# Two more weight sums of a seven-product pair made by accumulating DMAs, and the last convolution written stage by stage

## The chip, the cores and the metric

The kernel runs on one core of one Trainium2 chip. The metric is the device time of one execution in microseconds (us); lower is better. The engines named below are TensorE (PE; PEld is its weight load), VectorE (DVE), ScalarE (ACT), GpSimd (POOL) and SyncE (SP), which only issues transfers. Each engine runs its own instructions in order. Transfers issued by SP and by POOL go through separate queues and are carried by the same 16 DMA engines.

## The reference: what is computed

One decoder layer on x of 256 tokens by 2048 columns, all float32. The part that the change touches is the channel mixer: an up-projection to 2 x 5632 columns, a causal depthwise convolution of width 3, a gated GELU, and the down-projection.

```python
def causal_dwconv(u, w, b):
    S = u.shape[1]
    up = jnp.pad(u, ((0, 0), (CONV_WIDTH - 1, 0), (0, 0)))
    y = b
    for kk in range(CONV_WIDTH):
        y = y + up[:, kk:kk + S] * w[kk]
    return y
...
        x = x + rmsnorm(mix, post_mix_g[l])
        h = rmsnorm(x, pre_ffn_g[l])
        u = causal_dwconv(h @ w_up[l], conv_w[l], conv_b[l])
        gate, val = jnp.split(u, 2, axis=-1)
        y = (jax.nn.gelu(gate, approximate=True) * val) @ w_down[l]
        x = x + rmsnorm(y, post_ffn_g[l])
```

Ahead of it stand the pre-norm, the input projection (`w_in`), two groups of attention heads and the output projection (`w_out`).

## The kernel before

**Three matmuls for one.** Every float32 weight that is loaded into a `raw` buffer is split: ACT writes a rounded copy (`hi`), then DVE subtracts it from the weight (`lo`). A product of float32 accuracy is three matmuls: activation-high by `hi`, activation-high by `lo`, activation-low by `hi`. So each loaded unit of 128 x 1024 weights costs one ACT instruction, one DVE instruction and a pair of output tiles (`whi`/`wlo`, `slots`, or `more`, in which the second half of the layer has eight more places).

**Stages.** Attention and the projections around it fill the first 325 us or so. Then the feed-forward part runs in two halves of 22 blocks of 128 hidden columns. A half is a gate/up stage (11 groups g; for each the gate and the value columns are projected from `w_up`, convolved, passed through GELU, multiplied and split into the tiles `G`) and two column passes, which multiply the 22 blocks by columns 0 to 1023 and 1024 to 2047 of `w_down` (c0 is 0 or 1024). So there are four column passes.

**Seven products.** A pass goes over pairs u of blocks (k, k+1). Six of the eleven pairs (`FAST`) are done by seven products where eight are usual, as in Strassen's method in Winograd's form: tokens in two halves, the block pair as two rows, 512 columns each, so the weights form b11, b12 (row k, left and right) and b21, b22 (row k+1). With t1 = b11 + b12, t3 = b22 + b12, t2 = b22 + t1 and t4 = b21 + t2 the seven products multiply the tiles b11, (t1, t3), (b21, b22) and (t2, t4). A seven-product pair takes 7 x 3 = 21 matmuls of 512 columns, a plain pair 24.

**Where the sums come from.** t1 and t3 are made in DRAM long ahead, in a tile `t13` per pair: two copies from `w_down` by SP, then two accumulating transfers by POOL that add b12. These four steps per pair are put into the stream of weight loads by `w_load` (one step at every fifth load after the twelfth). In the pass itself `prepare` loads b11, (t1, t3) as `r13` and row k+1 as `r2`; (t2, t4) is then made on DVE by two additions of 128 x 512 over `r13` (L1025 and L1026), which wait for the split of `r13` to be done, and whose result is split in its turn.

**Order.** PE is ordered by hand everywhere. In the last group of a half and in the passes ACT, DVE and SP also go in the order of the code; elsewhere a scheduler orders them. A pass runs its pairs in a fixed order, for example 0, 2, 4, 1, 5, 6, 7, 3, 8, 9, 10 in the last one. After the last seven-product pair `early_sums` (L1141 to L1149) turns four accumulators into output columns: one ACT copy and eight DVE additions in the second half. The last pairs of a pass are held back and are multiplied bank by bank (`block`), and after each bank in the second half `down` (L1209, L1210) adds it on DVE and squares it on ACT.

**Convolution.** `conv_begin` (L921 to L929) takes for one block of 128 channels: an ACT copy, a DVE addition, a POOL multiplication, an ACT activation. `conv_end` has two DVE instructions. In the last group of a half it runs for the two value blocks one after the other, after the splits of the pass's first two plain pairs have been put in line.

Of the kernel before, what the change touches and what calls it, by code (L numbers as in the profile page):

```python
# [17 lines left out]
P = 128  # L18
S = 256
D = 2048  # L20
# [4 lines left out]
NEG = -1e30  # L25
FHALF = 22
HOLD = 3
EVERY, SKIP = 5, 12
FAST = (0, 2, 4, 5, 6, 7)


# [1 line left out]
def hybrid_layer(ctx: ExitStack, tc: tile.TileContext, x, pre_mix_g, w_in, b_forget, sinks,  # L33
# [33 lines left out]

    pair_sums, sum_steps, loads, paused = {}, [], [0], [False]

    def make_sums(key, k):  # L70
        t = tc.dram_tile([P, D], F32, name="t13")
        pair_sums[key] = t
        to = t.rearrange("p (s x c) -> p s x c", s=2, x=2)
        ups, downs = (w_down[(k + a) * P:(k + a + 1) * P, :]
                      .rearrange("p (s x c) -> p s x c", s=2, x=2) for a in range(2))
        return [lambda: sp.dma_start(to[:, :, 0, :], ups[:, :, 0, :]),
                lambda: sp.dma_start(to[:, :, 1, :], downs[:, :, 1, :]),
                lambda: pool.dma_start(to[:, :, 0, :], ups[:, :, 1, :], accum_op=ALU.add),
                lambda: pool.dma_start(to[:, :, 1, :], ups[:, :, 1, :], accum_op=ALU.add)]

    def w_load(src, a, c, pin=False):
        raw = wp.tile([P, UNIT], F32, tag="raw", bufs=5, name="raw")
        i = sp.dma_start(raw[:, :a * c].rearrange("p (a c) -> p a c", a=a), src)
        if pin:
            tc.keep_in_program_order(i)
        loads[0] += 1
        if loads[0] % EVERY == 0 and loads[0] > SKIP and sum_steps and not paused[0]:
            tc.keep_in_program_order(sum_steps.pop(0)())
        return raw, a, c

    for half in range(2):
        for u in FAST:
            sum_steps += make_sums((half, u), half * FHALF + 2 * u)


    LOW = 56

# [770 lines left out]
    with tc.tile_pool(name="ffn", bufs=1) as fp:  # L868
# [45 lines left out]
        y_sb = main.tile([P, 2, D], F32, tag="y", name="y_sb")  # L914

        def conv(b, ch, dst_tag):
            return conv_end(*conv_begin(b, ch, dst_tag))

        def conv_begin(b, ch, dst_tag):
            u = ubuf[cnt[0] % NU]  # L920
            cnt[0] += 1  # L921
            c = from_ring("cs")
            act.copy(c, b[:, 256:512])
            dve.tensor_tensor(u[:, 2:258], b[:, 0:256], c, op=ALU.add)  # L924
            pool.tensor_tensor(u[:, 2:258], u[:, 2:258], rowf, op=ALU.mult)  # L925
            y = from_ring(dst_tag)
            act.activation(y, u[:, 2:258], AF.Identity, bias=cw[:, 3, ch:ch + 1],  # L927
                           scale=cw[:, 2, ch:ch + 1])
            return u, y, ch  # L929
# [71 lines left out]
        def column_pass(G, sums, weights, some, order, k00, c0, load, parts, hold=1):  # L1001

            left, right = slice(0, 512), slice(512, UNIT)
            fast = [u for u in order if u in some]
            plain = [u for u in order[:-hold] if u not in some]
            ready, started, held, banks = {}, set(), [], []
# [9 lines left out]
            def prepare(u):  # L1016
                k = k00 + 2 * u
                if u not in some:
                    return [parts(load(w_rows(w_down, k + a, 1, c0, UNIT)), UNIT)
                            for a in range(2)]  # L1020
                b11 = parts(load(w_rows(w_down, k, 1, c0, 512)), 512)
                r13 = load(weights[u][:, c0:c0 + UNIT].rearrange("p (a c) -> p a c", a=1))
                r2 = load(w_rows(w_down, k + 1, 1, c0, UNIT))
                f13 = parts(r13, UNIT)
                dve.tensor_tensor(r13[:, left], r2[:, right], r13[:, left], op=ALU.add)  # L1025
                dve.tensor_tensor(r13[:, right], r2[:, left], r13[:, left], op=ALU.add)  # L1026
# [126 lines left out]
        for half in range(2):  # L1153
# [5 lines left out]
            for g in range(FHALF // 2):  # L1159
# [18 lines left out]
                if g == FHALF // 2 - 1:  # L1178
                    inner = tc.manual_schedule(engines={mybir.EngineType.Activation,
                                                        mybir.EngineType.DVE,  # L1180
                                                        mybir.EngineType.SP})
                    inner.__enter__()
                    passes = column_passes()
                    passes[0][0](1, 3)
                    begun = [conv_begin(bv[m], 44 + c0 // P + m, "yv") for m in range(2)]
# [142 lines left out]
```

## Time and profile before

| | |
|---|---|
| time, median of 3 runs (lowest to highest) | 1075.53 us (1075.0 to 1076.7) |
| time of the profiled execution | 1075.73 us |
| its span, first to last instruction | 1074.0 us |
| mean granted TensorE clock | 0.996 |
| busy: PE, DVE, ACT, POOL | 1048.1, 856.1, 647.6, 249.1 us |
| bytes moved by DMA | 238.56 MB, mean 222 GB/s |
| gate/up stage and two passes of the first half | from about 365 to 580 us, 580 to 695 us |
| gate/up stage and two passes of the second half | from 695 to 938 us, 938 to about 1064 us |

A row of the profile's groups reads: line, engine, operation, what is written and read, number of instructions, then busy time in us and mean ns of one, then the idle time of the engine just before them and what ended it. A row of a timeline reads: start, duration, engine, line, operation; in brackets the idle time before it and its releaser. A row of windows gives for a stretch of time the length, the busy time of each engine with the number of instructions in brackets, the clock granted to PE (1.00 is full), the busy share of the DMA engines and the GB/s. A matmul of 512 columns is listed with some 390 ns because matmuls overlap.

### The profile page before, as it was taken

To read this page: it belongs to the slowest core of one execution; us is meant where nothing else is said; L and a number is where in the kernel's file an instruction comes from. 1 tells how busy PE (TensorE), PEld (TensorE's weight loads), DVE (VectorE), ACT (ScalarE), POOL (GpSimd) and SP (SyncE) were. 2 spreads that over 40 slices of the span, in tenths; PEclk is the share of its full clock that TensorE was granted. 3 is DMA by queue.
4 is the path that set the end of the run, shared out by engine and by line. 5 is a ranking of instruction groups with operands and counts; after the bars stand their busy time and mean duration, and the time that the engine had idled before them with its cause. 6 is when DMAs were issued, how large, how long until landed. Compare 5 with 4: busy or idle time off the path is not lost.

```text
span 1074.0 us, 16449 instructions
## 1 busy us (share of the span) xinstructions
PE 1048.1 (98%) x5866; PEld 906.8 (84%) x5866; DVE 856.1 (80%) x1389; ACT 647.6 (60%) x1116; POOL 249.1 (23%) x280
## 2 busy tenths in 40 slices
PE   9999999999999999999999999999999999999895
PEld 7899988888889888888888787888888888878574
DVE  5988878887468788788776999867778887689895
ACT  7776757767457666566564656555556565565661
POOL 3253344440131122222221000012222222100005
PEclk9999999999999999999999999999999999999998
DMA  8749688675984998777876767768787766658482
GB/s 293 238 132 226 186 233 248 185 218 157 328 271 112 318 269 235 218 235 222 246 215 167 260 240 248 226 215 230 235 235 227 210 203 194 196 176 282 151 322 86
DMA packets 171230, 238.56 MB, mean 222 GB/s; under 512 B 8044, under 2 KB 132236, under 8 KB 170252
## 3 DMA queue, kind: packets, MB, share of 16 engines
q1 hardware_dynamic: 163616, 222.25, 64.6%
q0 software_dynamic: 6528, 12.58, 7.9%
q10 hardware_dynamic: 1004, 2.68, 0.6%
q8 instruction: 46, 0.75, 0.3%
q14 instruction: 36, 0.29, 0.1%
HBM read 233.14 MB, written 29.38 MB: 244 GB/s over the span
## 4 chain that ended last, share of the span: by engine, by line
PE 74%; DVE 13%; issue 5%; ACT 4%; DMA 2%; POOL 1%; SPq 0%; DVEq 0%; ACTq 0%; POOLq 0%
PE bank_acc L305 14%; PE bank_att L305 13%; PE bank_acc L330 12%; PE bank_acc L311 7%; PE bank_acc L274 7%; PE bank_att L311 7%; PE bank_acc L279 4%; PE bank_att L998 4%; DVE wlo L334 3%; DVE more L334 2%; DMA raw<-in_w_up_dram 1%; ACT whi L333 1%; DVE wlo L136 1%; PE bank_acc L998 1%; PE bank_att L496 1%
## 5 line engine op out<-in xcount | busy, mean ns | idle before, releaser
L136 DVE TENSOR_TENSOR wlo<-raw,whi 128x1024 fp32r<-128x1024 f32 (+3 forms) x271 | 332.3, 1238 | 114.5 <-ACT whi L133 106.6
L133 ACT CAST whi<-raw 128x1024 fp32r<-128x1024 f32 (+3 forms) x270 | 273.0, 1029 | 119.7 <-issue 66.1
L925 POOL TENSOR_TENSOR room<-room,rowf 128x256 f32<-128x256 f32 x88 | 98.9, 1142 | 372.1 <-DVE room L924 371.1
L305 PE MATMUL bank_acc<-hT,whi 128*128 128x512 f32 x736 | 173.3, 390 | 0.0
L305 PEld LDWEIGHTS bank_acc<-hT,whi 128*128 128x128 f32 x736 | 136.4, 188 | 27.4
L305 PE MATMUL bank_att<-hT,whi 128*128 128x512 f32 x640 | 150.6, 390 | 0.0
L305 PEld LDWEIGHTS bank_att<-hT,whi 128*128 128x128 f32 x640 | 118.7, 188 | 23.8
L998 PE MATMUL bank_att<-whi,G 128*128 128x512 f32 x298 | 98.1, 389 | 0.0
L927 ACT ACTIVATE room<-room,cw 128x256 f32<-128x256 f32 x88 | 52.9, 602 | 69.8 <-POOL room L925 69.8
L311 PEld LDWEIGHTS bank_acc<-hT,wlo 128*128 128x128 f32 x736 | 89.3, 188 | 2.0
L311 PE MATMUL bank_acc<-hT,wlo 128*128 128x256 f32 x736 | 89.9, 279 | 0.0
L274 PE MATMUL bank_acc<-hT,whi 128*128 128x512 f32 x352 | 88.0, 395 | 0.0
L330 PE MATMUL bank_acc<-whi,oT 128*128 128x512 f32 (+1 forms) x272 | 81.8, 379 | 0.0
L311 PEld LDWEIGHTS bank_att<-hT,wlo 128*128 128x128 f32 x640 | 77.7, 188 | 2.5 <-DVE wlo L136 0.8
L311 PE MATMUL bank_att<-hT,wlo 128*128 128x256 f32 x640 | 78.2, 279 | 0.6 <-DVE wlo L136 0.6
L932 DVE SCALAR_TENSOR_TENSOR room<-room,cw 128x256 f32<-128x256 f32 x88 | 61.3, 697 | 16.9 <-ACT room L927 16.9
L274 PEld LDWEIGHTS bank_acc<-hT,whi 128*128 128x128 f32 x352 | 63.3, 188 | 11.6
L334 DVE TENSOR_TENSOR wlo<-raw,whi 128x1024 fp32r<-128x1024 f32 (+1 forms) x61 | 65.8, 1107 | 6.7 <-ACT whi L333 6.1
L333 ACT CAST whi<-raw 128x1024 fp32r<-128x1024 f32 (+1 forms) x61 | 55.9, 955 | 21.3 <-DVE raw L1026 13.7
L998 PEld LDWEIGHTS bank_att<-whi,G 128*128 128x128 f32 x298 | 56.0, 188 | 11.4
L998 PE MATMUL bank_att<-wlo,G 128*128 128x512 f32 x149 | 58.9, 395 | 6.0 <-DVE wlo L334 6.0
L330 PEld LDWEIGHTS bank_acc<-whi,oT 128*128 128x128 f32 x272 | 50.2, 188 | 9.3
(269 smaller groups left out, 1723.0 us busy)
## 6 DMA issues: line engine op xcount, KB each, us to landing
raw<-in_w_up_dram SPq DMA_DIRECT2D x176, 512.0 KB, 4.6
raw<-in_w_in_dram SPq DMA_DIRECT2D x51, 512.0 KB, 5.4
raw<-in_w_down_dram SPq DMA_DIRECT2D x45, 512.0 KB, 5.0
raw<-in_w_out_dram SPq DMA_DIRECT2D x32, 512.0 KB, 5.9
t<-in_w_down_dram SPq DMA_DIRECT2D x24, 512.0 KB, 6.4
t<-in_w_down_dram POOLq DMA_DIRECT2D x24, 512.0 KB, 8.4
spare<-in_w_down_dram SPq DMA_DIRECT2D x14, 512.0 KB, 3.7
raw<-in_w_in_dram SPq DMA_DIRECT2D x16, 384.0 KB, 3.3
```

What stands on the lines that cost most here:

```text
L133: i1 = act.copy(hi[:, cs], raw[:, cs])
L136: i2 = dve.tensor_tensor(lo[:, cs], raw[:, cs], hi[:, cs].bitcast(F32), op=ALU.subtract)
L274: pe.matmul(b, parts[u][0][:, a, m * P:(m + 1) * P], hT[:, kt, :], start=(kt == 0), stop=(kt == KT - 1))
L305: pe.matmul(b, parts[u][0][:, a, m * P:(m + 1) * P], hT[:, kt, :], start=(kt == 0), stop=(kt == KT - 1))
L311: pe.matmul(b[:, 256:512], parts[u][1][:, a, m * P:(m + 1) * P], hT[:, kt, 0:256], start=False, stop=False)
L330: pe.matmul(b, a, r[:, cols], start=(first and i == 0), stop=(last and i == 2))
L333: act.copy(hi, src)
L334: dve.tensor_tensor(lo, src, hi.bitcast(F32), op=ALU.subtract)
L925: pool.tensor_tensor(u[:, 2:258], u[:, 2:258], rowf, op=ALU.mult)
L927: act.activation(y, u[:, 2:258], AF.Identity, bias=cw[:, 3, ch:ch + 1], scale=cw[:, 2, ch:ch + 1])
L932: dve.scalar_tensor_tensor(y, u[:, 1:257], cw[:, 1, ch:ch + 1], y, op0=ALU.mult, op1=ALU.add)
L998: pe.matmul(b[:, to] if to else b, a, r[:, cols], start=(first and i == 0), stop=(last and i == 2))
```

## The change

The table of steps is longer: each pair has a second DRAM tile `t24`. SP copies b22 to its left and b21 to its right half, then POOL adds t1 from `t13` to the left half and the left half to the right one, all in DRAM, so t2 and t4 are ready before the pass. For the pairs of the first half only columns 0 to 1023 are made (half-size transfers of 256 KB). That is 8 steps per pair and 96 in all, where there were 48. The rule for putting them in line goes from one step at every fifth load to five at every 13 loads. The last step of a pair is put behind the first two of the next pair.

Three passes (`ready_sums`: the first pass of the first half, both of the second) load (t2, t4) as a unit of its own, `r24`, and have no DVE additions. The second pass of the first half still adds on DVE, with row k+1 now always split ahead of (t2, t4). `conv_begin` takes a list of blocks and goes stage by stage through both.

```diff
-    def make_sums(key, k):
-        t = tc.dram_tile([P, D], F32, name="t13")
...
+    def make_sums(half, u):
+        k = half * FHALF + 2 * u
+        chunks = slice(0, 2) if half else slice(0, 1)
+        t13, t24 = (tc.dram_tile([P, D], F32, name=n) for n in ("t13", "t24"))
+        pair_sums[half, u] = t13, t24
...
+        return [put(t1, b11), put(t3, b22), add(t1, b12), add(t3, b12), put(t2, b22, chunks),
+                put(t4, b21, chunks), add(t2, t1, chunks), add(t4, t2, chunks)]
...
-        if loads[0] % EVERY == 0 and loads[0] > SKIP and sum_steps and not paused[0]:
+        if loads[0] > SKIP and loads[0] * 5 % 13 < 5 and sum_steps and not paused[0]:
             tc.keep_in_program_order(sum_steps.pop(0)())
...
+            steps = make_sums(half, u)
+            sum_steps += steps[:2] + last + steps[2:7]
+            last = steps[7:]
+    sum_steps += last
...
+        def conv_begin(blocks):
+            us, cs = [], []
+            for b, _, _ in blocks:
...
+                act.copy(cs[-1], b[:, 256:512])
+            for (b, _, _), u, c in zip(blocks, us, cs):
+                dve.tensor_tensor(u[:, 2:258], b[:, 0:256], c, op=ALU.add)
+                pool.tensor_tensor(u[:, 2:258], u[:, 2:258], rowf, op=ALU.mult)
...
+            for (_, ch, tag), u in zip(blocks, us):
+                y = from_ring(tag)
+                act.activation(y, u[:, 2:258], AF.Identity, bias=cw[:, 3, ch:ch + 1],
...
+            ready_sums = k00 or c0 == 0
...
-                dve.tensor_tensor(r13[:, left], r2[:, right], r13[:, left], op=ALU.add)
-                dve.tensor_tensor(r13[:, right], r2[:, left], r13[:, left], op=ALU.add)
-                if u == fast[0]:
-                    f24 = parts(r13, UNIT)
-                    return b11, f13, parts(r2, UNIT), f24
+                if ready_sums:
+                    r24 = load(w24)
+                else:
+                    r24 = r13
+                    dve.tensor_tensor(r24[:, left], r2[:, right], r13[:, left], op=ALU.add)
+                    dve.tensor_tensor(r24[:, right], r2[:, left], r24[:, left], op=ALU.add)
                 b2 = parts(r2, UNIT)
-                return b11, f13, b2, parts(r13, UNIT)
+                return b11, f13, b2, parts(r24, UNIT)
```

PE's instructions stand in the same order in both kernels. On DVE, the start of the first pass of the second half stood like this (pair 0 and the first tiles of pair 2; `slots`, `more` and `wlo` are the low parts, `extra` and `raw` the loaded weights):

```order
L334 TENSOR_TENSOR wlo<-raw,whi 128x512
L334 TENSOR_TENSOR slots<-extra,slots 128x1024
L1025 TENSOR_TENSOR extra<-raw,extra 128x512
L1026 TENSOR_TENSOR extra<-raw,extra 128x512
L334 TENSOR_TENSOR more<-extra,more 128x1024
L334 TENSOR_TENSOR more<-raw,more 128x1024
L334 TENSOR_TENSOR more<-raw,more 128x512
```

In the changed kernel the same place, whose lines are numbered ten higher, reads:

```order
L344 TENSOR_TENSOR wlo<-raw,whi 128x512
L344 TENSOR_TENSOR slots<-extra,slots 128x1024
L344 TENSOR_TENSOR more<-raw,more 128x1024 x2
L344 TENSOR_TENSOR more<-raw,more 128x512
L344 TENSOR_TENSOR more<-raw,more 128x1024
```

The two additions are gone, and (t2, t4) is split from a buffer of its own behind row k+1. On SP, the last loads of `w_out` and the first of `w_up` stood like this (`t` is a sum tile in DRAM):

```order
L83 DMA raw<-in_w_out_dram 128x2x512 x5
L77 DMA t_78<-in_w_down_dram 256x512
L83 DMA raw<-in_w_up_dram 128x4x256 x10
L76 DMA t_79<-in_w_down_dram 256x512
L83 DMA raw<-in_w_up_dram 128x4x256 x5
L77 DMA t_79<-in_w_down_dram 256x512
L83 DMA raw<-in_w_up_dram 128x4x256 x15
```

They now stand like this:

```order
L90 DMA raw<-in_w_out_dram 128x2x512 x8
L90 DMA raw<-in_w_up_dram 128x4x256 x2
L80 DMA t_83<-in_w_down_dram 128x512
L90 DMA raw<-in_w_up_dram 128x4x256 x3
L80 DMA t_83<-in_w_down_dram 128x512
L90 DMA raw<-in_w_up_dram 128x4x256 x5
L80 DMA t_84<-in_w_down_dram 256x512
L90 DMA raw<-in_w_up_dram 128x4x256 x2
L80 DMA t_84<-in_w_down_dram 256x512
L90 DMA raw<-in_w_up_dram 128x4x256 x11
```

Two half-size copies are new in this stretch, and the second full-size one comes three loads earlier. On ACT, the last convolution of a half was:

```order
L923 COPY room<-bank_acc 128x256
L927 ACTIVATE room<-room,cw 128x256
L923 COPY room<-bank_acc 128x256
L927 ACTIVATE room<-room,cw 128x256
L333 CAST G_7427<-room 128x256
```

and is now:

```order
L935 COPY room<-bank_acc 128x256 x2
L942 ACTIVATE room<-room,cw 128x256 x2
L343 CAST G_7470<-room 128x256
```

Both copies now stand ahead of both activations; DVE's rows there are in the same order as before.

More of the change, by code (lines that the diff above doesn't have):

```diff
@@ L27 @@
 HOLD = 3
-EVERY, SKIP = 5, 12
+SKIP = 12
 FAST = (0, 2, 4, 5, 6, 7)
@@ L86, in w_load @@
         loads[0] += 1
-        if loads[0] % EVERY == 0 and loads[0] > SKIP and sum_steps and not paused[0]:
+        if loads[0] > SKIP and loads[0] * 5 % 13 < 5 and sum_steps and not paused[0]:
             tc.keep_in_program_order(sum_steps.pop(0)())
         return raw, a, c
+    last = []
     for half in range(2):
         for u in FAST:
-            sum_steps += make_sums((half, u), half * FHALF + 2 * u)
+            steps = make_sums(half, u)
+            sum_steps += steps[:2] + last + steps[2:7]
+            last = steps[7:]
+    sum_steps += last
     LOW = 56
@@ L1184, in hybrid_layer @@
                     passes[0][0](1, 3)
-                    begun = [conv_begin(bv[m], 44 + c0 // P + m, "yv") for m in range(2)]
+                    begun = conv_begin([(bv[m], 44 + c0 // P + m, "yv") for m in range(2)])
                 for m in range(2):
```

39 lines of the change are left out of this document (18 added, 21 removed).

## The prediction

> **What bounds the kernel now.** I read the busy shares first, then how far PE falls behind its own pace in each column pass, then who releases it there. PE is the bound overall:
>
> ```profile
> PE 1048.1 (98%) x5866; PEld 906.8 (84%) x5866; DVE 856.1 (80%) x1389; ACT 647.6 (60%) x1116; POOL 249.1 (23%) x280
> ```
>
> "Busy" hides short waits, so I count matmuls. This row of the chain of waits (start, length, count) is a stretch without waits:
>
> ```profile
> 678.49 17.00 PE bank_att L998 x75
> ```
>
> That is 17.00/75 = 0.2267 us for a matmul of 512 columns. A pass has 6 seven-product and 5 plain pairs, 6 x 21 + 5 x 24 = 246 matmuls, so 55.8 us without waits. The windows below are cut at each pass's first matmul; the last pass is cut once more after its last seven-product pair (150 matmuls, 34.0 us) and after its first held-back bank (24 + 18 matmuls, 9.5 us):
>
> ```profile
> 580.08:638.65 58.57, 56.90 (x248) 45.94 (x246) 52.27 (x63) 33.64 (x42) 1.56 (x2) 1.00 0.67 228
> 638.65:695.33 56.68, 56.10 (x248) 46.10 (x246) 50.38 (x55) 30.94 (x35) 0.20 (x4) 1.00 0.75 243
> 937.77:996.04 58.27, 56.56 (x247) 45.76 (x246) 53.03 (x65) 31.11 (x39) 1.55 (x2) 1.00 0.64 217
> 996.04:1037.11 41.07, 36.27 (x152) 27.84 (x151) 37.29 (x41) 27.43 (x36) 0.00 (x0) 1.00 0.64 217
> 1037.11:1051.30 14.19, 10.46 (x43) 7.42 (x42) 13.92 (x16) 4.89 (x6) 3.65 (x2) 1.00 0.71 262
> ```
>
> Lost to waits are 2.8, 0.9, 2.5, 7.1 and 4.7 us, 18.0 in all (each first column less its ideal). DVE, the third busy column, is at 89 to 98% there, and PE's waits from 925 us on name it (total us, times, longest):
>
> ```profile
> PE bank_att L998 <- DVE wlo L334: 4.5, 5, 2.1
> PE bank_acc L998 <- DVE more L334: 1.9, 4, 0.8
> ```
>
> In a run of seven-product pairs DVE is slower than PE. Its timeline shows the first addition of three pairs:
>
> ```profile
> 1020.01 0.69 DVE L1025 TENSOR_TENSOR raw<-raw 128x512 f32<-128x512 f32 x1
> 1020.74 0.69 DVE L1026 TENSOR_TENSOR raw<-raw 128x512 f32<-128x512 f32 x1
> 1025.63 0.69 DVE L1025 TENSOR_TENSOR spare<-spare 128x512 f32<-128x512 f32 x1
> 1031.24 0.69 DVE L1025 TENSOR_TENSOR raw<-raw 128x512 f32<-128x512 f32 x1
> ```
>
> A pair costs DVE 5.6 us (1025.63 to 1031.24) and PE 21 x 0.2267 = 4.76.
>
> **The change, part by part.** *Additions removed.* Each costs its spacing, 1020.74 - 1020.01 = 0.73 us; two leave a seven-product pair with 5.6 - 1.45 = 4.15 us on DVE, below PE's 4.76. Is ACT next? Four splits and their means:
>
> ```profile
> L333 ACT CAST whi<-raw 128x1024 fp32r<-128x1024 f32 (+1 forms) x35 | 31.9, 949 | 9.3 <-DVE raw L1026 6.4 <-issue 2.8
> L333 ACT CAST whi<-raw 128x512 fp32r<-128x512 f32 x2 | 1.2, 616 | 0.0
> ```
>
> Even at 1.05 us for a full cast (the row of 35 mixes in half-size ones) a pair is 3 x 1.05 + 0.62 = 3.8 us, also under PE, and ACT no longer waits for L1026. So inside a run of pairs nothing but transfers can hold PE. In the two first passes I leave 0.3 us each of their 2.8 and 2.5: gain 2.5 + 2.2 = 4.7. The second pass of the first half keeps its additions and its 0.9.
>
> *The second half's change of pass.* PE there waited for DVE and ACT in turn:
>
> ```profile
> 985.77 0.58 ACT L1141 COPY s<-bank_acc 128x512 f32<-128x512 f32 x1
> 987.79 0.68 DVE L1142 TENSOR_TENSOR y_sb<-s,y_sb 128x512 f32<-128x512 f32 x1
> 1000.13 2.48 DVE L1209 TENSOR_TENSOR y_sb<-bank_att,y_sb 128x512 f32<-128x512 f32 x4
> 1000.87 1.66 PE L998 MATMUL bank_att<-more,G 128*128 128x512 f32 x6 [1.00 <-DVE y_sb L1209]
> 1004.39 0.50 PE L998 MATMUL bank_acc<-more,G 128*128 128x512 f32 x1 [1.18 <-ACT more L333]
> 1008.09 1.57 ACT L333 CAST whi<-raw 128x1024 fp32r<-128x1024 f32 x2 [1.85 <-PE bank_acc L998]
> ```
>
> In the old time scale the new order runs so. DVE, no longer behind, starts the eight sums when the ACT copy ends, 986.4, and ends them 8 x 0.72 = 5.8 us later, at 992.1. Four low parts of pair 0 follow (about 4.1 us: 996.2), then the four `down` additions (2.5 us: 998.7). PE starts pair 0 at 996.04, needs the bank of the third `down` after 12 matmuls, at 998.8, and finds it free. ACT squares behind each `down` until about 1000.0 and only then casts pair 2: 1000.6, 1001.6, 1002.6, 1003.5. PE wants that pair at 1000.8 and waits some 0.4 us for its first and 0.9 us for its second low part. I keep 1.5 of the 7.1: gain 5.6.
>
> *The end.* Here the eight sums stand between the last seven-product pair and four low parts that the held-back banks need:
>
> ```profile
> 1039.54 0.68 DVE L1142 TENSOR_TENSOR y_sb<-s,y_sb 128x512 f32<-128x512 f32 x1
> 1046.43 0.50 PE L998 MATMUL bank_att<-wlo,G 128*128 128x512 f32 x1 [2.13 <-DVE wlo L334]
> 1050.92 0.74 PE L998 MATMUL bank_att<-more,G 128*128 128x512 f32 x2 [1.26 <-DVE more L334]
> ```
>
> The order stays; only DVE's backlog ahead of the sums goes. They could start at 1038.1 rather than 1039.54, end at 1043.9, and the low parts at about 1048.5, so the bank ends near 1049.2 where it ended at 1051.3. I take 1.9 and leave 2.8 of the wait. Together 4.7 + 5.6 + 1.9 = 12.2 us.
>
> *The convolution.* The activations of both blocks can end about 1.4 us earlier, DVE's low part of the first pair about 1.0. Two plain pairs (10.9 us of matmuls) cover all this, so it is worth nothing beside the 0.3 above; with DVE still behind it would be worth up to 1.0 twice.
>
> *Transfers in the passes.* (t2, t4) adds 0.52 MB to a seven-product pair: 0.26 + 3 x 0.52 = 1.83 MB, which PE uses up in 4.76 us, 385 GB/s; a plain pair asks for 1.05 MB in 5.44 us, 193 GB/s. Busy stretches elsewhere reached:
>
> ```profile
> 290.00:300.00 10.00, 10.00 (x46) 8.29 (x45) 6.04 (x5) 6.38 (x8) 0.00 (x0) 1.00 0.97 343
> 355.00:360.00 5.00, 5.00 (x25) 4.16 (x24) 4.36 (x6) 4.97 (x9) 0.91 (x1) 1.00 1.03 365
> ```
>
> At 343 GB/s a seven-product pair takes 5.35 us, 0.6 more than PE; three in a row fall 1.8 us back, and a plain pair gives 2.4 back (3.06 against 5.44). Eight raw buffers hold two pairs ahead, so I take 0, and keep the uncovered price for the rivals.
>
> *Transfers in the stages ahead.* 48 more steps, 24 half-size. The gate/up stages show the share of the DMA engines (the column before the last) with steps in the first two rows, without in the third:
>
> ```profile
> 365.00:565.00 200.00, 199.36 (x1161) 176.16 (x1160) 163.40 (x255) 122.07 (x194) 47.60 (x43) 1.00 0.81 237
> 695.00:875.00 180.00, 180.00 (x1042) 158.92 (x1041) 139.93 (x213) 105.24 (x164) 42.02 (x38) 1.00 0.77 223
> 875.00:933.00 58.00, 58.00 (x345) 51.52 (x345) 46.01 (x72) 35.09 (x56) 11.71 (x11) 1.00 0.64 192
> ```
>
> A load comes every 2.75 us (eight in a group of 22.0 us), so 180 us hold 13 steps: (0.77 - 0.64) x 180/13 = 1.8 us of all engines a step, and 2.4 us in the first half's stage. The new rate, 5 steps in 35.8 us, makes 0.64 + 5 x 1.8/35.8 = 0.89, and 0.97 at 2.4; first-half steps are partly half-size. Under 1, but narrowly. Below nothing this cost cannot go; above, the queues give the bound:
>
> ```profile
> q1 hardware_dynamic: 163616, 222.25, 64.6%
> q0 software_dynamic: 6528, 12.58, 7.9%
> L78 POOL DMA_DIRECT2D t<-in_w_down_dram x12 | 11.1, 924 | 0.0
> ```
>
> An accumulating transfer holds the engines for 0.079 x 1074/24 = 3.5 us, a copy of the same size for about 1.6 (0.646 x 1074/222 x 0.52). On POOL, 24 more issues at 0.92 us stand before convolution and residual work; ACT's activations are behind that, and PE behind ACT, with five split buffers between. POOL idles three quarters of the time; I take 1.2 us for all of this, near the end that the measured share supports.
>
> By the Trainium skill (DMA: Bandwidth & Descriptors, Queues, rings and completion order) an engine goes round-robin between queues packet by packet, so a load beside an accumulating transfer should take up to twice as long. The trace agrees in part: medians to landing of 6.7 us with one and 4.4 without.
>
> ```profile
> raw<-in_w_up_dram SPq DMA_DIRECT2D x8, 512.0 KB, 6.7
> raw<-in_w_up_dram SPq DMA_DIRECT2D x14, 512.0 KB, 4.4
> ```
>
> Five buffers of 2.75 us, 13.8 us, cover 6.7.
>
> *New waits.* The accumulating transfer of t2 waits on POOL for its copy and for t1, the one of t4 for t2. Queued behind it are convolution multiplications (earlier in the program residual gains), for which ACT's activations wait, and behind those ACT's casts for PE. Landing takes:
>
> ```profile
> t<-in_w_down_dram SPq DMA_DIRECT2D x24, 512.0 KB, 6.4
> t<-in_w_down_dram POOLq DMA_DIRECT2D x24, 512.0 KB, 8.4
> ```
>
> Steps are 2.6 loads, 7.2 us, apart in a gate/up stage; t4 follows t2 by three steps, t2 its copy by two, so both medians are over before POOL asks. If one were not, some 8 us less 7 would be lost, once a pair, behind a convolution that is not due for a group of 22 us. I price the waits at nothing beyond the 1.2. SP gets 24 more copies of about 0.5 us issue time between loads that are 2.75 us apart; covered too. In the pass the load of `r24` waits for sums that were done at about load 262 (12 + 96 x 2.6) of 281, 50 us ahead.
>
> **Sum.** The profiled execution took 1075.7 us, its span 1074.0, the median of the runs 1075.5. 1075.7 - 12.2 + 1.2 = 1064.7, on the median's scale 1064.5.
>
> **Rivals.** *A: transfers bound the passes.* If buffers come free too late to run ahead, 18 pairs lose 0.6 us each, 10.6: 1075. With the plain pairs giving half back, 1070. For: 385 GB/s is more than any stretch shows. Against: DMA was busy 0.64 to 0.75 in the passes. By the Trainium skill (same page, Specifications) HBM gives a core about 358 GB/s; by that a pair takes 5.1 us, and without any lead the time would be 1071. The 365 GB/s above do not contradict it for longer stretches.
>
> *B, slower: the doubled steps saturate DMA in the gate/up stages.* Some 34 steps fall in the first and 26 in the second, 12 groups of five. It costs as soon as five steps need more than 0.36 x 35.8 = 12.9 us, 2.6 each, and passes the gain at about 2.8. If each cost 3.0, 5 x 3.0 - 12.9 = 2.1 us a group: 25 us, 1089. For: 0.97 above, and the stage from 345 us on is saturated already. Against: 1.8 in the longer clean stretch.
>
> *C: the waits move.* In the last two places ACT's squares, or sums and low parts in DVE's order, keep twice what I left: 1069.
>
> *D: no change.* PE's waits are taken up by loads that arrive late everywhere: within 0.2% of 1075.5 (2.2 us, about what can be told from no change).
>
> **Numbers.** Forecast 0.63, A 0.12, C 0.11, B 0.08, D 0.06. Faster: 0.63, C, and nearly all of A, 0.85; same 0.06; slower 0.09. The range is 1060.5 (all 18 us of waits less 3) to 1072 (A by half and C inside).
>
> **What would show it.** Right: DVE below 50 us in the three passes; the stretch to the last seven-product pair near 35.5 us, the one after it near 12; no PE wait on DVE inside runs of pairs; gate/up stages as long as before with DMA near 0.9. Wrong: PE waits on transfers in runs of pairs (A), on splits waiting for loads at 345 to 400 or in the later gate/up stage (B), on ACT behind L1210's successors (C).

## The result and the profile after

The changed kernel takes 1060.85 us (median of 4 runs, 1058.93 to 1065.77) beside 1075.45 us; the ratio is 0.9869 with a 95% interval of 0.9833 to 0.9906. The profiled execution took 1059.58 us, its span is 1057.9. In a later comparison it took 1059.03 us (5 runs, 1058.47 to 1061.08) beside 1077.11 for the kernel before, ratio 0.9827 (0.9806 to 0.9848). In the three sets of experiments, each on a chip of its own, the kernel before has medians of 1078.75, 1078.22 and 1077.11 us, with single runs 6 to 8 us apart within a set. So below times are compared within a set, and single microseconds are read from windows of the profiled executions.

The busy shares, which answer to the first row of the prediction:

```profile
PE 1043.1 (99%) x5866; PEld 907.9 (86%) x5866; DVE 836.6 (79%) x1353; ACT 651.9 (62%) x1116; POOL 265.7 (25%) x304
```

The windows of the changed kernel are these: both passes of the first half, the first of the second half, the last up to its last seven-product pair, and its first held-back bank.

```profile
580.82:636.58 55.76, 55.76 (x247) 46.17 (x246) 47.21 (x54) 35.37 (x42) 1.34 (x2) 1.00 0.83 304
636.58:692.34 55.76, 55.76 (x247) 46.17 (x246) 47.78 (x51) 30.96 (x35) 1.10 (x5) 1.00 0.78 254
934.78:990.54 55.76, 55.76 (x247) 46.17 (x246) 48.81 (x56) 36.53 (x46) 1.34 (x2) 1.00 0.80 303
990.54:1024.54 34.00, 34.00 (x151) 28.15 (x150) 29.50 (x29) 27.21 (x33) 0.00 (x0) 1.00 0.93 342
1024.54:1035.53 10.99, 9.84 (x44) 7.81 (x43) 10.78 (x12) 2.46 (x3) 3.64 (x2) 1.00 0.67 272
```

Three passes and the greater part of the fourth now run at exactly PE's own pace: 55.76 is 246 x 0.2267, and 34.00 is 150 x 0.2267. From 575 us to the end PE's waits have a single row left:

```profile
PE bank_att L1014 <- DVE more L344: 1.2, 1, 1.2
```

Two boundaries of the prediction's windows lie one matmul early: the last pass of the kernel before begins at 996.26 us, not 996.04, and its first held-back bank ends at 1051.51, not 1051.30. At the same matmuls as in the changed kernel its last three windows are:

```profile
937.77:996.26 58.49, 56.78 (x248) 45.95 (x246) 53.25 (x65) 31.11 (x39) 1.55 (x2) 1.00 0.65 217
996.26:1037.11 40.85, 36.05 (x151) 27.65 (x150) 37.07 (x41) 27.43 (x36) 0.00 (x0) 1.00 0.64 217
1037.11:1051.51 14.40, 10.67 (x44) 7.58 (x43) 14.09 (x16) 4.89 (x6) 3.86 (x2) 1.00 0.70 258
```

So its waits there were 2.7, 6.9 and 4.9 us where the prediction has 2.5, 7.1 and 4.7, and 18.2 us in all where it has 18.0. The gain in the two profiled executions, window by window, is 58.57 - 55.76 = 2.81; 56.68 - 55.76 = 0.92; 58.49 - 55.76 = 2.73; 40.85 - 34.00 = 6.85; 14.40 - 10.99 = 3.41; and in the tail behind the first bank 22.49 - 22.37 = 0.12. Against them stands that the first pass starts at 580.82 where it started at 580.08, 0.74 later. The sum, 16.84 - 0.74 = 16.10, is the whole difference of the spans, 1074.0 - 1057.9.

The gate/up stages got no longer. The second one is 242.44 us long in both kernels (695.33 to 937.77 before, 692.34 to 934.78 after), with the DMA engines much busier:

```profile
365.74:565.74 200.00, 200.00 (x1168) 176.97 (x1168) 163.22 (x254) 119.30 (x188) 54.28 (x51) 1.00 0.93 261
692.34:872.00 179.66, 179.66 (x1040) 158.64 (x1039) 139.50 (x213) 105.17 (x164) 46.26 (x44) 1.00 0.89 254
```

The 0.74 us arise before the first gate/up stage. Followed matmul by matmul, the changed kernel is 0.18 us late after the first 12 us; it loses 1.51 us where the residual is added and transposed for the up-projection (19.07 us from 322 us on, where the kernel before took 17.56); and it gets 0.9 us back behind 364 us, where a wait of 0.6 us on DVE is gone. Among PE's waits up to 580 us these two are longer than before or new (before, the longest for `x_in` was 0.6 us):

```profile
PE bank_acc L365 <- DMA x_in<-in_x_dram: 0.9, 1, 0.9
PE bank_att L794 <- DVE x_sb L787: 0.6, 1, 0.6
```

### The profile page after: what moved, and what is told of

Its sections match the earlier page's. It is cut to its first block, busy times and chain, and to the rows that moved or that the text cites. A ratio compares the mean times of both kernels' runs of the same rounds, so it can differ in the third digit from the quotient of the medians.

```text
span 1057.9 us, 16559 instructions
## 1 busy us (share of the span) xinstructions
PE 1043.1 (99%) x5866; PEld 907.9 (86%) x5866; DVE 836.6 (79%) x1353; ACT 651.9 (62%) x1116; POOL 265.7 (25%) x304
## 4 chain that ended last, share of the span: by engine, by line
PE 84%; DMA 5%; DVE 5%; issue 2%; ACT 2%; POOL 1%; SPq 0%; DVEq 0%; POOLq 0%; ACTq 0%
PE bank_acc L315 16%; PE bank_att L315 14%; PE bank_att L1014 11%; PE bank_acc L321 8%; PE bank_att L321 7%; PE bank_acc L284 7%; PE bank_acc L340 7%; PE bank_acc L1014 5%; PE bank_acc L289 4%; DMA raw<-in_w_out_dram 3%; PE bank_att L506 1%; DVE wlo L146 1%; PE bank_att L541 1%; DMA raw<-t 1%; PE bank_acc L977 1%
## 5 line engine op out<-in xcount | busy, mean ns | idle before, releaser
L146 DVE TENSOR_TENSOR wlo<-raw,whi 128x1024 fp32r<-128x1024 f32 (+3 forms) x271 | 336.6, 1254 | 109.0 <-ACT whi L143 101.1
L938 POOL TENSOR_TENSOR room<-room,rowf 128x256 f32<-128x256 f32 x88 | 96.5, 1116 | 357.6 <-DVE room L937 356.2
```

The source lines that it names most:

```text
L146: i2 = dve.tensor_tensor(lo[:, cs], raw[:, cs], hi[:, cs].bitcast(F32), op=ALU.subtract)
```

## The experiments

This table has all runs whose profile could be used. The first column is the median time; the others are lengths in each profiled execution, cut at the same matmuls: start of the first column pass, the two passes of the first half (A, B), the second gate/up stage, then in the second half the first pass (C), the last pass to its last seven-product pair (D) and its first held-back bank (E). All in us.

| kernel | time | start | A | B | gate/up | C | D | E |
|---|---|---|---|---|---|---|---|---|
| no waits (count x 0.2267) | | | 55.8 | 55.8 | | 55.8 | 34.0 | 9.5 |
| before | 1075.5 | 580.08 | 58.57 | 56.68 | 242.44 | 58.49 | 40.85 | 14.40 |
| changed | 1060.85 | 580.82 | 55.76 | 55.76 | 242.44 | 55.76 | 34.00 | 10.99 |
| changed, second profile | 1059.03 | 582.34 | 55.76 | 55.76 | 242.44 | 55.76 | 34.00 | 10.97 |
| no additions | 1060.16 | 580.01 | 55.76 | 55.76 | 242.44 | 55.76 | 34.00 | 11.80 |
| steps only | 1071.62 | 580.16 | 56.48 | 55.76 | 242.44 | 56.37 | 40.08 | 14.38 |
| old convolution | 1059.67 | 579.98 | 55.76 | 55.76 | 242.44 | 55.76 | 34.00 | 10.88 |
| order of splits only | 1071.57 | 579.60 | 57.41 | 55.76 | 242.44 | 57.31 | 40.12 | 14.32 |
| last pass only | 1064.20 | 580.91 | 56.48 | 55.76 | 242.44 | 56.41 | 36.13 | 11.64 |
| dense steps | 1070.35 | 581.57 | 55.76 | 55.76 | 250.18 | 55.76 | 34.00 | 10.86 |
| low parts first | 1059.21 | 582.12 | 55.76 | 55.76 | 242.44 | 55.76 | 34.00 | 9.52 |
| low parts first, again | 1058.19 | 581.22 | 55.76 | 55.76 | 242.44 | 55.76 | 34.00 | 9.52 |
| second half only | 1061.89 | 583.06 | 56.50 | 55.76 | 242.44 | 55.76 | 34.00 | 9.52 |
| order alone, no transfers | 1066.63 | 580.68 | 56.49 | 55.76 | 242.44 | 56.41 | 40.06 | 9.52 |

### No additions, no transfers

From the kernel before:

```diff
                 f13 = parts(r13, UNIT)
-                dve.tensor_tensor(r13[:, left], r2[:, right], r13[:, left], op=ALU.add)
-                dve.tensor_tensor(r13[:, right], r2[:, left], r13[:, left], op=ALU.add)
                 if u == fast[0]:
```

> The kernel before without its two DVE additions a pair, and without any new transfer; t2 and t4 are left out (t1 and t3 are split a second time in their place), so the output is not the reference's. Theory (the additions alone are what the column passes waited for): the waits of all four passes go as in the changed kernel, 16.5 us of the 18.0, and the 0.74 us that the changed kernel loses ahead of 580 us is not paid: 1075.5 - 16.5 = 1059.0, and the runs lie within 2 us as those of the kernel before do. Rival 1 (the second pass of the first half gained by the new order of its splits, the change of pass by the convolution): 1061 to 1063. Rival 2 (the last pass waits for something other than DVE): above 1065.

Measured: 1060.16 us (1058.9 to 1060.3), ratio 0.9843 (0.9817 to 0.9868). The theory held. The 48 additions are enough to explain every wait in A to D: with nothing else changed the windows have the changed kernel's lengths to the hundredth. PE's waits there had no other cause, the one of 1.18 us put down to ACT included. E stays 0.8 us longer than in the changed kernel; why was not sought.

```profile
989.73:1023.73 34.00, 34.00 (x151) 28.15 (x150) 28.90 (x29) 28.40 (x35) 0.00 (x0) 1.00 0.81 284
1023.73:1035.53 11.80, 10.37 (x44) 7.65 (x43) 11.59 (x12) 0.50 (x1) 3.95 (x2) 1.00 0.47 181
```

### Steps only

From the changed kernel:

```diff
-            ready_sums = k00 or c0 == 0
+            ready_sums = False
```

> The changed kernel with all 96 steps, but every pass adds on DVE as the kernel before does; the new sums are never read. Theory (the steps cost what PE lost ahead of 580 us, 0.74 us, and nothing in the gate/up stages): 1075.5 + 0.7 = 1076.2, less 0.9 if the order of the splits is what helped the second pass of the first half. Rival (the steps cost more than the profile of one execution shows, the spread of the changed kernel being theirs): 1078 to 1082, with runs several us apart.

Measured: 1071.62 us (1069.89 to 1075.14), ratio 0.9945 (0.9929 to 0.996). This was a miss for both: with all the new transfers and every addition in place the kernel is faster than before, by 4 to 8 us by the interval. Its windows A, B, C:

```profile
580.16:636.64 56.48, 56.38 (x247) 46.01 (x246) 53.02 (x64) 33.76 (x42) 1.34 (x2) 1.00 0.70 231
636.64:692.40 55.76, 55.76 (x247) 46.17 (x246) 49.29 (x54) 30.96 (x35) 1.10 (x5) 1.00 0.77 253
934.84:991.21 56.37, 56.27 (x247) 46.02 (x246) 52.83 (x65) 32.08 (x40) 1.34 (x2) 1.00 0.68 225
```

So in these three passes the additions could stay: 5.1 of the 6.5 us that the passes gained in the changed kernel also come without leaving them out. Two edits are left that can have done it, the order of the splits and the convolution.

### Convolution only, and the old convolution in the changed kernel

The first is the kernel before with the changed kernel's `conv_begin`; the second is the changed kernel with the `conv_begin` of before:

```diff
-                    begun = conv_begin([(bv[m], 44 + c0 // P + m, "yv") for m in range(2)])
+                    begun = [conv_begin(bv[m], 44 + c0 // P + m, "yv") for m in range(2)]
```

> The kernel before with the last convolution stage by stage and nothing else. Theory (two plain pairs cover it): within 0.5 us of 1075.5. Rival (with DVE behind, the first passes gain up to 1.0 us each): 1073.5.

> The changed kernel with the convolution of the kernel before, one block after the other. Theory: nothing, the median of the changed kernel, 1060.9 within its spread, and first passes of 55.8 us. Rival: the first passes lose 0.5 to 1.0 us each, 1062 to 1063.

Measured: convolution only 1074.0 us, ratio 0.9969 (0.9952 to 0.9987), a gain of 1.4 to 5.2 us. Its profiled execution took 3724.26 us, where the eleven others took 1072.57 to 1077.96; the reason is open, it is left out, and so this kernel has no windows. The theory (no effect) fell for the kernel before. Old convolution 1059.67 us (1058.66 to 1060.01), and A and C of 55.76: in the changed kernel the edit is worth nothing. Both fit the reading that a lead on DVE is worth its length while DVE is behind, and nothing once it is not.

### Order of the splits only

From the kernel before:

```diff
-                if u == fast[0]:
-                    f24 = parts(r13, UNIT)
-                    return b11, f13, parts(r2, UNIT), f24
                 b2 = parts(r2, UNIT)
                 return b11, f13, b2, parts(r13, UNIT)
```

> The kernel before with one edit: the split of row k+1 goes ahead of the split of (t2, t4) in a pass's first seven-product pair too, as in the changed kernel. Additions, convolution and transfers stay. Theory (in the kernel before DVE stood 1.18 us there for ACT's cast of (t2, t4); that time comes back as lead): the first passes lose 1.2 us less each, the second pass of the first half its 0.9, the last pass 1 to 2 less: 4 to 5 us, 1071 beside 1075.5. Rival (the convolution gave the steps-only kernel its gain): 1074.5 to 1075.5.

Measured: 1071.57 us (1070.96 to 1074.25), ratio 0.9949 (0.993 to 0.9968). The theory held, but for the last pass, which got 0.7 us shorter and not 1 to 2. The timeline of DVE at the first seven-product pair of the first pass shows it, first in the kernel before:

```profile
591.17 0.69 DVE L1026 TENSOR_TENSOR extra<-raw,extra 128x512 f32<-128x512 f32 x1
593.04 1.23 DVE L334 TENSOR_TENSOR wlo<-extra,whi 128x1024 fp32r<-128x1024 f32 x1 [1.18 <-ACT whi L333]
```

and with row k+1 (`raw`) ahead of (t2, t4) (`extra`):

```profile
590.68 0.69 DVE L1026 TENSOR_TENSOR extra<-raw,extra 128x512 f32<-128x512 f32 x1
591.29 1.22 DVE L334 TENSOR_TENSOR wlo<-raw,whi 128x1024 fp32r<-128x1024 f32 x1
592.55 1.23 DVE L334 TENSOR_TENSOR wlo<-extra,whi 128x1024 fp32r<-128x1024 f32 x1
```

DVE no longer stands for 1.18 us while ACT casts what DVE has just added. That is all of B's loss, 1.2 us each of A and C, and 0.7 of D. The convolution then adds 57.41 - 56.49 = 0.92 in A and 57.31 - 56.41 = 0.90 in C, as the row "order alone" shows against this one: up to the end of C the two kernels differ in the convolution alone.

### Only the last pass reads ready sums

From the changed kernel:

```diff
-            ready_sums = k00 or c0 == 0
+            ready_sums = k00 and c0
```

> The changed kernel, all steps made, but only the second pass of the second half reads (t2, t4) ready made; the three others add on DVE. Theory (the order of splits and the convolution free the other passes, the additions only matter in the last one): passes of 56.3, 55.9 and 55.8 us, the last one as in the changed kernel, 1060.5 to 1061.5. Rival (the last pass gains because DVE enters it without a backlog from the pass before): 1063 to 1067.

Measured: 1064.20 us (1063.65 to 1066.2), ratio 0.9879 (0.9859 to 0.9899). The rival held; D is 36.13, not 34.00, though A and B went as the theory said (C took 56.41 where it had 55.8):

```profile
992.00:1028.13 36.13, 34.87 (x151) 28.00 (x150) 31.96 (x33) 28.44 (x37) 0.00 (x0) 1.00 0.93 335
1028.13:1039.77 11.64, 10.21 (x43) 7.65 (x42) 11.34 (x13) 3.13 (x3) 3.60 (x2) 1.00 0.72 294
```

DVE, behind in the pass before, ends its early sums at 989.24, 2.8 us ahead of the last pass, has four low parts to do, and its `down` additions start after that pass has begun (at 992.00); in the changed kernel they start 2.5 us ahead of it (988.02 against 990.54):

```profile
988.55 0.69 DVE L1169 TENSOR_TENSOR y_sb<-s,y_sb 128x512 f32<-128x512 f32 x1
993.17 2.48 DVE L1229 TENSOR_TENSOR y_sb<-bank_att,y_sb 128x512 f32<-128x512 f32 x4
```

So D's 6.85 us, taken in this order, split into three: 0.7 for the order of the splits (40.85 to 40.1), 4.0 for the last pass's own additions (40.1 to 36.13), and 2.1 for those of the passes before, which lengthen C itself by only 0.6 us.

### Denser steps

From the changed kernel (`late[0]` is set at the start of the second half):

```diff
-        if loads[0] > SKIP and loads[0] * 5 % 13 < 5 and sum_steps and not paused[0]:
+        if loads[0] > SKIP and sum_steps and not paused[0] and (
+                loads[0] * 2 % 3 < 2 if late[0] else
+                loads[0] * 5 % 13 < 5 and len(sum_steps) > 48):
```

> The changed kernel with the first half's 48 steps as they are, the second half's 48 held back to the second gate/up stage and put there at two of three loads, where the changed kernel has five of thirteen (8.7 steps in 35.8 us for 5). The rows of the changed kernel give 1.8 us of all DMA engines a step, (0.89 - 0.64) x 179.66/25. Theory (nothing is lost until the engines are full, then all of the excess): 0.64 x 198 + 48 x 1.8 = 213 us of transfers in the 198 us of 72 loads, 15 us late, less the 10 us or so that five buffers run ahead: 5 to 15 us more than the changed kernel, PE waiting on splits that wait for loads. Rival (2.6 to 3.0 us a step, rival B of the forecast): 50 us more or above. Rival (the share of busy time overstates what a step costs the loads): no difference.

The break after 48 steps puts the t4 addition of the first half's last pair into the second half, so that pair's product with t4 uses b21 alone. Measured: 1070.35 us (1067.95 to 1074.44), ratio 0.9936 (0.9913 to 0.996). The gate/up stage grew by 250.18 - 242.44 = 7.74 us and everything else kept its length; the theory held, both rivals fell. The window and PE's waits in it:

```profile
693.09:903.09 210.00, 203.95 (x1172) 178.90 (x1171) 154.66 (x240) 117.01 (x184) 53.27 (x56) 1.00 1.04 286
```

```profile
PE bank_att L324 <- DVE wlo L149: 3.2, 4, 1.6
PE bank_acc L324 <- DVE wlo L149: 1.6, 1, 1.6
PE bank_att L318 <- ACT whi L146: 1.3, 1, 1.3
```

The DMA engines are full (1.04), the median landing of a `w_up` load in this stage is 9.5 us where it is 4.5 in the changed kernel, and splits come late. The 1.8 us of all engines per step are therefore about right, and the loss that rival B described is real once the engines are full; the changed kernel stays below that, with 0.89 and 0.93. Where between 0.93 and 1.04 it begins was not tried.

### Low parts first

From the changed kernel, the last pass only (`hold` is 3 there): the splits of the last four pairs go ahead of the eight sums on ACT and DVE.

```diff
                         if u == fast[-1]:
-                            ahead(*order[i + 1:i + 3])
+                            ahead(*order[i + 1:i + (5 if hold > 1 else 3)])
                             add_early(*early)
```

> The changed kernel with the splits of all four last pairs of the last pass ahead of the eight sums on ACT and DVE, so that the 1.15 us wait of PE on the last low part goes. Theory: 1.1 us less than the changed kernel, 1058.5 to 1059.5, if DVE ends the sums (now about 1034.3 in the changed kernel's time scale) when the first held-back bank ends. Rival: the sums end later and the tail after the first bank is longer by what the bank gains; no difference.

Measured: 1059.21 us (1058.56 to 1059.61), ratio 0.9829 (0.9807 to 0.985). E is 9.52, no wait at all. To compare it with the changed kernel on one chip both were run again:

> The changed kernel, unaltered, for a second profile and for times beside the three below. Theory (its four first runs lie 7 us apart by chance; its column passes are free of waits in every execution): 1059.5 to 1061, passes of 55.8 us, a start of the first pass between 580 and 582 us. Rival (the added transfers make its time waver): runs up to 1066 again, with PE waiting on splits that wait for loads.

> The changed kernel with the last four splits ahead of the eight sums, a second time, beside the changed kernel on the same chip. Theory: 1.4 us less (the first held-back bank took 9.5 us where it takes 10.9 to 11.0), with the tail of about 22.4 us as before. Rival: the two within 0.3 us of each other.

Measured: the changed kernel 1059.03 us (1058.47 to 1061.08), ratio 0.9827 (0.9806 to 0.9848), this one 1058.19 us (1057.41 to 1058.89), ratio 0.9821 (0.98 to 0.9842). The medians differ by 0.8 us and the intervals overlap; the windows say 10.97 - 9.52 = 1.45 us here and 10.99 - 9.52 = 1.47 the first time, with tails of 22.34 and 22.54 us beside 22.37. Low parts first has the lowest median of the study. The second profile of the changed kernel has the column passes of the first, and times that lie closer together than those of the kernel before (1075.2 to 1081.78); that its transfers make the time waver is not borne out. Its one run of 1065.77 has no profile and stays unexplained.

```profile
1024.94:1034.46 9.52, 9.52 (x43) 7.89 (x42) 7.93 (x9) 3.58 (x4) 1.56 (x2) 1.00 0.79 322
1034.46:1056.80 22.34, 12.63 (x73) 11.02 (x71) 14.75 (x24) 3.19 (x10) 10.99 (x10) 0.86 0.26 94
```

### Ready sums in the second half only

From the kernel with low parts first:

```diff
-SKIP = 12
+SKIP = 60
...
+        return steps if half else steps[:4]
...
-            ready_sums = k00 or c0 == 0
+            ready_sums = k00
```

> As the one above, but with (t2, t4) ready made in the second half alone: the first half's 24 half-size steps are left out, its two passes add on DVE, and the steps begin at load 61 instead of 13. Theory (the first half's additions cost its first pass 0.72 us, as in the steps-only kernel; early steps cost the stages ahead about 1 us of late loads): first pass starting at 579.6 to 580.1 us, passes of 56.5, 55.8, 55.8 and 55.8 us, the time within 0.5 us of the kernel with the last four splits first. Rival (early steps cost nothing, the start wavers by itself): 0.7 us slower than that one.

Measured: 1061.89 us (1061.25 to 1064.14), ratio 0.986 (0.9837 to 0.9882), 3.7 us slower than low parts first. A came out as expected; the start did not: at 583.06 it is the latest of all. Both theory and rival fell. Among PE's waits up to 580 us:

```profile
PE bank_att L323 <- DVE wlo L148: 1.8, 2, 1.1
```

The two waits lie at 367.01 and 378.84 us, behind the stretch in which the DMA engines were already full in the kernel before (355 to 360 us in the prediction). Between 260 and 365 us this kernel issues 12 steps of 512 KB; of the 12 in the changed kernel 5 are of 256 KB. So the later start put more bytes into the one stretch that had no room, though not many (27.2 MB where it was 26.8). That this is the cause was not tried apart.

### Order alone

From the kernel before: the order of the splits, the new `conv_begin` and low parts first, each as above; no new transfer, all additions on DVE.

> The kernel before with three edits of order and no new transfer: row k+1 split first, the convolution stage by stage, the last four splits ahead of the eight sums. All additions stay on DVE. Theory: passes of 56.5, 55.8 and 56.4 us and 40.1 us to the last seven-product pair as in the steps-only kernel; the first held-back bank loses 1 to 2 us instead of 4.9, since DVE comes to it late: 1066 to 1067. Rival (what the bank gains comes back as sums that end late): 1069 to 1070.

Measured: 1066.63 us (1064.84 to 1068.56), ratio 0.9899 (0.988 to 0.9918). The theory held:

```profile
991.78:1031.84 40.06, 35.92 (x152) 27.69 (x150) 37.10 (x41) 26.49 (x35) 0.00 (x0) 1.00 0.64 222
1031.84:1041.36 9.52, 9.52 (x44) 7.88 (x42) 8.96 (x10) 4.88 (x6) 0.00 (x0) 1.00 0.95 356
1041.36:1065.40 24.04, 12.63 (x73) 11.02 (x71) 16.24 (x27) 3.19 (x10) 12.95 (x11) 0.86 0.28 101
```

E goes to 9.52, and 1.7 us of it come back in the tail (24.04 beside 22.34). Beside 1077.1 this kernel gains 10.5 us and the changed one 18.1, so more than half of that time can be had by order. One of the three orders, low parts first, is not in the changed kernel: the two that are took 5.9 us out of A to E (steps only), where the whole change took 16.7. What no order of this study gave is D, where DVE alone has 37.1 us of work in 40.1.

## Why the prediction was right, and where it was not

**The bound.** Right: PE's lost time in the passes was DVE's, all but 1.5 us of it is gone, and leaving the additions out alone does it.

**Additions removed, 4.7 us in the two first passes.** Measured 2.81 + 2.73 = 5.5; the remainder of 0.3 us each did not stay. The size was nearly right, the reason only half: the additions' removal is enough for these passes, but so, to within 0.7 and 0.6 us, are the two edits of order. With causes that each suffice, the step could not be read from the trace of before by the additions' price alone.

**The second pass of the first half keeps its 0.9.** Wrong; it is gone. The step that failed is one that the working left out: that row k+1 is split first was stated as part of the change, and not priced. DVE's 1.18 us wait for ACT's cast stood in the timeline of before, in each pass's first seven-product pair.

**Change of pass, 5.6 of 7.1.** Measured 6.85, which is all that was lost there. The term was mis-sized because the hand schedule let the eight sums start "when the ACT copy ends, 986.4", as if that copy were fixed. ACT had itself been waiting for DVE's additions: in the kernel before it stood 2.14 us for one, and from there worked without a break up to the copy at 985.77.

```profile
981.01 1.05 ACT L333 CAST more<-raw 128x1024 fp32r<-128x1024 f32 x1 [2.14 <-DVE raw L1026]
```

In the changed kernel the copy starts 990.54 - 976.35 = 14.2 us ahead of the pass's end, where it was 996.26 - 985.77 = 10.5:

```profile
976.35 0.57 ACT L1161 COPY s<-bank_acc 128x512 f32<-128x512 f32 x1
...
992.15 1.56 ACT L343 CAST more<-raw 128x512 fp32r<-128x512 f32 x2
```

```profile
977.62 0.69 DVE L1162 TENSOR_TENSOR y_sb<-s,y_sb 128x512 f32<-128x512 f32 x1
...
988.02 2.05 DVE L1229 TENSOR_TENSOR y_sb<-bank_att,y_sb 128x512 f32<-128x512 f32 x3
990.74 0.69 DVE L1229 TENSOR_TENSOR y_sb<-bank_att,y_sb 128x512 f32<-128x512 f32 x1 [0.67 <-PE bank_att L1014]
```

Three of the four `down` additions are over before the pass ends, ACT's squares end at 992.2, and the 1.5 us that were kept for them never arise: rival C fell.

**The end, 1.9 of 4.7.** Measured 3.4, for the same reason. The copy that started 0.4 us after the last seven-product pair now starts 2.3 us ahead of its end (1024.54), and the sums 1.0 us ahead of it. What is left is the order that the prediction named: the sums stand between, and PE waits 1.15 us for the last low part. First the copy in the kernel before, then in the changed one; then its first sum, and PE's wait:

```profile
1037.52 0.58 ACT L1141 COPY s<-bank_acc 128x512 f32<-128x512 f32 x1
```

```profile
1022.27 0.58 ACT L1161 COPY s<-bank_acc 128x512 f32<-128x512 f32 x1
```

```profile
1023.54 0.69 DVE L1162 TENSOR_TENSOR y_sb<-s,y_sb 128x512 f32<-128x512 f32 x1
```

```profile
1034.95 0.74 PE L1014 MATMUL bank_att<-more,G 128*128 128x512 f32 x2 [1.15 <-DVE more L344]
```

**Convolution, nothing; "with DVE still behind it would be worth up to 1.0 twice".** Right in both halves: 0 in the changed kernel, 0.92 and 0.90 with the additions in place.

**Transfers in the passes, 0; rival A.** Right, rival A fell. In the runs of seven-product pairs the loads came at the pace that PE asked for, and faster than in any stretch of that length in the kernel before (at most 339 GB/s over 28 us and 383 over 14):

```profile
948.00:976.00 28.00, 28.00 (x125) 23.20 (x124) 25.15 (x24) 21.76 (x24) 0.00 (x0) 1.00 1.02 403
1010.00:1024.00 14.00, 14.00 (x63) 11.59 (x62) 13.16 (x12) 12.13 (x14) 0.00 (x0) 1.00 1.02 414
```

PE was busy for all of both. The 343 GB/s from which the step took 0.6 us a pair was that of a stretch of other transfers, not a limit. The 358 GB/s that the Trainium skill gives a core (DMA: Bandwidth & Descriptors, Specifications) are passed for 28 us; where it says that a core which streams alone measures about 425 (HBM Reference, Specifications (TRN2)), the trace agrees in that its 403 and 414 lie between the two.

**Steps in the stages ahead, 1.2 us; rival B.** The size came out about right, the place did not. The forecast shares of 0.89 to 0.97 came out at 0.89 and 0.93 without a wait in either gate/up stage, and the price is paid ahead of them: the first pass starts at 581.1 us in the mean of seven executions with the changed kernel's steps (579.98 to 582.34) and at 580.1 in the four without (579.60 to 580.68). Much of that spread is not the steps' doing: the same matmul comes at 11.1 to 12.4 us in kernels of both kinds, long before the first step is issued at 32 us. The stretch of the residual separates them better. It takes 17.56 us in each of the four executions without the steps, and 17.56 to 19.07 us, 18.4 in the mean, in the eight with them (the denser steps are the same up to there). Rival B did not happen, and its mechanism was shown by the denser steps. The landing of 6.7 us beside an accumulating transfer, which the working covers with five buffers, is near the slow end: over the groups of 22 us from 695 to 915 us in the kernel before, the medians of the `w_up` loads are 4.4 to 7.0 us with such a transfer and 3.8 to 4.5 without.

**New waits on POOL and SP, 0.** Wrong ahead of the gate/up stages, right inside them. Where the residual is formed, POOL has three accumulating transfers to issue, in front of two multiplications, where the kernel before had one. POOL's `rmix` comes later, DVE waits longer for it, and PE waits 0.6 us for DVE's `x_sb`. First the kernel before, then the changed one:

```profile
317.94 0.89 POOL L78 DMA_DIRECT2D t<-in_w_down_dram  x1
322.91 2.74 DVE L777 SCALAR_TENSOR_TENSOR x_sb<-mix_sb,rmix,x_sb 128x512 f32<-128x512 f32 x4 [1.55 <-POOL rmix L204]
```

```profile
319.04 0.80 POOL L83 DMA_DIRECT2D t<-t  x1
319.59 2.06 POOL L83 DMA_DIRECT2D t<-in_w_down_dram  x2
324.77 2.74 DVE L787 SCALAR_TENSOR_TENSOR x_sb<-mix_sb,rmix,x_sb 128x512 f32<-128x512 f32 x4 [2.72 <-POOL rmix L214]
```

In the eight executions with the steps DVE waits 1.6 to 2.8 us there, in the four without 1.54 or 1.55. The working had named POOL's issues ahead of the residual, but let ACT hand the delay on and put it into the 1.2 us; it went through DVE. No run moved these issues, so this is read from the traces and was not tried.

**The sum.** It was 1064.5, and the time 1060.85, 3.7 less: 0.8 in the first passes, 0.9 in the second pass of the first half, 1.3 at the change of pass, 1.5 at the end, 0.1 in the tail and 0.5 of the steps' price, 5.1 in the profiled execution. The median lies 1.3 above that execution, and 0.2 were taken off in the forecast's step to the median's scale. Of the signs that the prediction named, DVE below 50 us came true (47.2, 47.8 and 48.8), while the last two stretches took 34.0 and 11.0 us, not 35.5 and 12. The time lies only 0.35 us above the lower end of the range, and the later median, 1059.03, lies below that end, because each wait was given a remainder that an engine with slack did not leave. That the first median, of four runs 7 us apart, falls inside is in part luck; the direction and the cause are not.

## What to carry to other kernels

When an engine that has fallen behind is relieved, do not hold the start of the next step fixed at the time that another engine's instruction had in the old trace: ask whether that instruction was itself waiting for the relieved engine. Before work is moved to other resources, look for places where the late engine stands still for something that it has just asked for (here about 1.2 us in each pass for a cast of its own result); reordering alone gave 10.5 us where the change gave 18.1. The gate/up stages here took the added transfers for nothing with the DMA engines at 0.93 busy, and lost 7.7 us at 1.04. What the transfers did cost came from the engine that issues them, so look at what stands behind an issue there.

## What was not expected of the hardware

In the last pass the time from its first matmul to its last seven-product pair was 40.1 us in three kernels in which DVE is the bound, whatever clock PE was granted (the column after POOL's): 0.96 in the kernel with the order of the splits only and in the one with steps only, 1.00 in the one with order alone, whose row stands above (40.06).

```profile
992.52:1032.64 40.12, 37.13 (x152) 28.66 (x150) 37.15 (x41) 26.53 (x35) 0.00 (x0) 0.96 0.65 220
```

```profile
991.21:1031.29 40.08, 37.21 (x151) 28.77 (x150) 37.12 (x41) 26.49 (x35) 0.00 (x0) 0.96 0.65 221
```

So the lower clock that shows in two of these stretches does not explain their length.
